# A hybrid trunk layer on one core: in-projection weight loads issued from ScalarE's queue, norm sums later, last activations kept in SBUF

## The chip, the cores and the metric

One core of a Trainium2 chip runs one program. The time of a run is device microseconds of that program; the time of a kernel is the median of its runs. The kernel before took 1511.74 us (three runs: 1519.3, 1505.03 and 1511.74).

## The reference

One layer over a sequence of 1024 steps and 1024 channels, in float32, and a last norm:

```python
h = rmsnorm(x, ln1_g[l])
p = h @ w_in[l]
pm, pr, pw = jnp.split(p, [M_COLS, M_COLS + R_COLS], axis=-1)
ym = mlstm_group(pm, ...)
yr = retention_group(pr)
yw = rwkv7_group(pw, ...)
y = jnp.concatenate([ym, yr, yw], axis=-1).astype(x.dtype)
x = x + y @ w_out[l]
h = rmsnorm(x, ln2_g[l])
x = x + (jax.nn.silu(h @ w_gate[l]) * (h @ w_up[l])) @ w_down[l]
...
return rmsnorm(x, lnf_g)
```

`rmsnorm` divides by the root of the mean square over the channels. The hidden width D_FF is 2816, 22 blocks of 128. The three groups are recurrences over time: mLSTM with 4 heads, retention with 6, RWKV-7 with 6, of 64 channels each.

## The kernel before, in words

**Precision.** Every operand of a large product is kept as two numbers, hi and lo. `split_hi` (L89, one ScalarE activation at L90) rounds to fp32r, `split_lo` (L92, one VectorE subtraction at L93) takes the rest, and a product is three matmuls: hi by hi, hi by lo, lo by hi. In the profile the weights are `whi` and `wlo`, the activations `act` and `act2`.

**Weight loads.** `w_part` (L99 to L102) takes one of three buffers named `wraw`, issues a load of 256 KB on SP's queue (L101), and returns it; `w_split` (L104) makes whi and wlo. A buffer is free for the next load when VectorE has made its wlo. The loads of w_cm and w_tm (the columns of w_in by channel and by time), of w_out and of w_down pass here, 210 in all. Gate and up weights have buffers of their own, `rg`, two of 1 MB, which the loads of hidden activations in the last stage use too.

**Stages.** Time is cut into two halves h of 512 steps, held as free elements of a tile; the partitions are channels.

1. From 0 to about 760 us: in-projection, the three mixers, and the out-projection of half 0. The order of the work is made by `weave` (L131, called at L1127), which takes generators in turn by a clock of its own and by named events; the instructions then run in that order on each engine. In the RWKV part, `rwkv_chain` carries a state over chunks (L581 to L600: matmuls into `chain`, copies `pm` at L583, `X` at L592 and L593 and `yw` at L610 on ScalarE). `rwkv_inverse` (L500) solves triangular systems: E goes to DRAM as `ab_d` (L497), comes back as `MN` (L507), is copied to `R` on ScalarE (L509), is worked on by VectorE (L514 to L522), and goes by `r_d` (L528) back into E (L532). It runs six times; every one of these transfers is issued on SP. So are the stores of the token-wise projections (`v_dram`, L760).
2. From about 760 to 830 us: the out-projection of half 1 (`out_tile`, L1033), eight tiles of 24 matmuls (L119 to L121) with steps of two generators put between each six matmuls: `second_norm(0)` (L1068) and `first_half`, which prepares operands for the next stage. `second_norm` has `rms_stats` (L155: matmuls of the summed squares `sqa` with ones at L159, a mean `ms` on VectorE at L161, a power `rs` on POOL at L162) and, two steps later, `rms_expand` (L164: matmuls at L166 that spread the factors to `misc`) and a copy to `RS`. The summed squares come from POOL (L1049). `second_half(d)` (L1154) makes further operands of tile d by subtractions on POOL and VectorE and by splits. After the last tile the first products of gate and up begin (`product`, L1171 to L1173), with copies named `pre` (L1432) and with the steps of `second_norm(1, 4)` between.
3. From about 830 to 1245 us: gate and up products of a scheme that needs seven products of half-size blocks in place of eight. Each hidden block of a half is stored to `a_dram` (L1181), but for the last two blocks of half 0, which stay in SBUF: `DIRECT` (L1185).
4. From about 1245 us to the end: the down-projection, for each half eight tiles of 22 x 3 matmuls (L1364 to L1366 into `chain`). `take` (L1307) makes its operands: it loads four blocks at a time from `a_dram` into `rg` (L1324) and splits them in pairs, or splits the tiles kept in SBUF. The residuals come back as `x3` (L1359), in buffers shared with the `work` tiles of stage 3.

**Order of the queues.** On each engine instructions run in program order, and a transfer waits on the queue of the engine that issues it: what stands behind it there waits too.

## Time and profile before

| what | us |
|---|---|
| median of three runs | 1511.74 |
| lowest and highest | 1505.03, 1519.3 |
| the profiled execution, its own time | 1521.67 |
| its span | 1519.9 |
| TensorE (PE) busy | 1425.6 |
| VectorE (DVE) busy | 892.4 |
| ScalarE (ACT) busy | 556.2 |
| GpSimd (POOL) busy | 437.9 |

The profile is one execution. A row of a group or a timeline names the line, the engine, the operation and what it writes and reads; a number in brackets is how long the engine sat idle before it and what ended that. PEld is the loading of TensorE's stationary operand, beside the matmuls. SPq and ACTq are issues of transfers. The granted clock is the share of full speed that TensorE was given: at full clock 512-column matmuls follow each other by 0.23 us, at half clock (0.50) by 0.43.

### The profile page before, as it was taken

The page shows a single profiled execution, that of the slowest core. Times are in us where ns is not written, and L with a number is a line of the kernel's source. Part 1 is how long each engine was busy: PE and PEld are TensorE (multiplying, and loading weights), DVE is VectorE, ACT ScalarE, POOL GpSimd, SP SyncE. Part 2 cuts the span into 40 slices and gives each one's busy share as a digit, 9 for nine tenths or more (in the row PEclk, how much of TensorE's full clock was granted, in tenths as well). Part 3 has the DMA queues.
Part 4 walks back from the last instruction along what each step waited for, and adds up shares of the span by engine and source line. Part 5 has one row for each costly group of instructions (what it writes and reads, how often), then busy time and mean ns, then how long its engine had stood idle before and what let it go on. Part 6 is the DMA issues. An engine that isn't in the chain of part 4 may idle for free.

```text
span 1519.9 us, 23085 instructions
## 1 busy us (share of the span) xinstructions
PE 1425.6 (94%) x8434; PEld 1161.3 (76%) x8434; DVE 892.4 (59%) x1762; ACT 556.2 (37%) x1202; POOL 437.9 (29%) x539
## 2 busy tenths in 40 slices
PE   7998799789998998999998999999999998999996
PEld 5777577777777887887777887888888886887886
DVE  6457567458847756645468555555555565347434
ACT  6353334333432133244456333333333344224222
POOL 3211013234424333333545433344444420000000
PEclk9999999999978889899999999999999999999998
DMA  5142122334422244354632222222222247337333
GB/s 209 43 136 66 50 80 74 83 89 112 122 59 68 85 129 124 106 161 142 220 112 85 96 83 83 72 73 78 83 84 83 83 168 255 93 95 238 98 97 111
DMA packets 122269, 164.55 MB, mean 108 GB/s; under 512 B 38028, under 2 KB 70956, under 8 KB 120876
## 3 DMA queue, kind: packets, MB, share of 16 engines
q1 hardware_dynamic: 122156, 163.08, 33.5%
q8 instruction: 66, 1.08, 0.3%
q14 instruction: 47, 0.39, 0.1%
HBM read 124.75 MB, written 38.29 MB: 107 GB/s over the span
## 4 chain that ended last, share of the span: by engine, by line
PE 53%; DVE 3%; POOL 2%; DMA 2%; issue 1%; ACT 0%; POOLq 0%; DVEq 0%; SPq 0%; ACTq 0%
PE acc L1171 5%; PE acc L1172 5%; PE acc L1173 5%; PE chain L1365 5%; PE chain L1364 5%; PE chain L1366 5%; PE misc L1172 4%; PE misc L1171 4%; PE misc L1173 4%; PE acc L119 2%; PE acc L121 2%; PE acc L120 2%; DVE act L93 1%; PE acc L729 1%; PE acc L731 1%
## 5 line engine op out<-in xcount | busy, mean ns | idle before, releaser
L93 DVE TENSOR_TENSOR wlo<-wraw,whi 128x512 fp32r<-128x512 f32 (+1 forms) x210 | 147.9, 707 | 138.3 <-ACT whi L90 137.1
L90 ACT ACTIVATE whi<-wraw 128x512 fp32r<-128x512 f32 (+1 forms) x210 | 128.1, 612 | 226.3 <-PE chain L1365 117.9
L729 PE MATMUL acc<-whi,act 128*128 128x256 f32 (+1 forms) x512 | 161.3, 318 | 4.4 <-ACT whi L90 3.4
L90 ACT ACTIVATE whi<-rg 128x512 fp32r<-128x512 f32 x128 | 79.8, 631 | 228.7 <-POOL rg L1232 90.0
L730 PE MATMUL acc<-wlo,act 128*128 128x256 f32 (+1 forms) x512 | 155.4, 305 | 5.2 <-DVE wlo L93 5.2
L119 PE MATMUL acc<-act,whi 128*128 128x512 f32 x352 | 152.3, 433 | 7.0 <-ACT whi L90 6.2
L93 DVE TENSOR_TENSOR wlo<-rg,whi 128x512 fp32r<-128x512 f32 x128 | 93.1, 728 | 108.1 <-ACT whi L90 105.9
L731 PE MATMUL acc<-whi,act 128*128 128x256 f32 (+1 forms) x512 | 153.0, 300 | 0.0
L1364 PE MATMUL chain<-act,whi 128*128 128x512 f32 (+1 forms) x374 | 144.3, 386 | 4.0 <-ACT act L90 4.0
L120 PE MATMUL acc<-act,whi 128*128 128x512 f32 x352 | 145.5, 413 | 1.5 <-DVE act L252 1.5
L121 PE MATMUL acc<-act,wlo 128*128 128x512 f32 x352 | 145.7, 414 | 1.1 <-DVE wlo L93 1.1
L1365 PE MATMUL chain<-act,whi 128*128 128x512 f32 (+1 forms) x374 | 144.0, 385 | 0.5 <-DVE act L93 0.5
L1366 PE MATMUL chain<-act,wlo 128*128 128x512 f32 (+1 forms) x374 | 143.8, 384 | 0.0
L1171 PE MATMUL acc<-act,whi 128*128 128x512 f32 x352 | 139.3, 396 | 3.4 <-ACT pre L1432 2.7
L1173 PE MATMUL acc<-act,wlo 128*128 128x512 f32 x352 | 138.8, 394 | 0.0
L1172 PE MATMUL acc<-act,whi 128*128 128x512 f32 x352 | 138.5, 394 | 0.0
L729 PEld LDWEIGHTS acc<-whi,act 128*128 128x128 f32 x512 | 104.3, 205 | 12.1 <-ACT whi L90 3.9
L730 PEld LDWEIGHTS acc<-wlo,act 128*128 128x128 f32 x512 | 105.0, 206 | 9.2 <-DVE wlo L93 6.7
L731 PEld LDWEIGHTS acc<-whi,act 128*128 128x128 f32 x512 | 105.2, 206 | 1.0
L1172 PE MATMUL misc<-act,whi 128*128 128x512 f32 x264 | 104.1, 394 | 0.0
L1171 PE MATMUL misc<-act,whi 128*128 128x512 f32 x264 | 104.0, 394 | 0.0
L1173 PE MATMUL misc<-act,wlo 128*128 128x512 f32 x264 | 103.8, 393 | 0.0
(327 smaller groups left out, 2835.9 us busy)
## 6 DMA issues: line engine op xcount, KB each, us to landing
wraw<-in_w_down SPq DMA_DIRECT2D x85, 256.0 KB, 2.7
rg<-in_w_gate SPq DMA_DIRECT2D x22, 512.0 KB, 4.9
rg<-in_w_up SPq DMA_DIRECT2D x22, 512.0 KB, 5.0
a_dram<-work SPq DMA_DIRECT2D x41, 256.0 KB, 2.2
wraw<-in_w_tm SPq DMA_DIRECT2D x40, 256.0 KB, 3.0
rg<-a_dram SPq DMA_DIRECT2D x10, 1024.0 KB, 6.1
v_dram<-vt SPq DMA_DIRECT2D x64, 128.0 KB, 1.9
wraw<-in_w_out SPq DMA_DIRECT2D x32, 256.0 KB, 3.2
```

The source lines that it names most:

```text
L90: S.activation(hi, src, AF.Copy, scale=scale)
L93: (eng or V).tensor_tensor(lo, src, hi.bitcast(F32), ALU.subtract)
L119: PE.matmul(ps, lhsT=hi, rhs=xh[:, k, :], start=(k == 0), stop=False)
L729: PE.matmul(o, lhsT=xh[h][:, k, sl], rhs=w[k][0], start=(k == 0), stop=False)
L730: PE.matmul(o, lhsT=xh[h][:, k, sl], rhs=w[k][1], start=False, stop=False)
L731: PE.matmul(o, lhsT=xl[h][:, k, sl], rhs=w[k][0], start=False, stop=(k == KT - 1))
L1171: PE.matmul(ps, lhsT=hi, rhs=hi_x[:, k, :], start=(start and k == 0), stop=False, skip_group_check=True)
L1172: PE.matmul(ps, lhsT=hi, rhs=lo_x[:, k, :], start=False, stop=False, skip_group_check=True)
L1173: PE.matmul(ps, lhsT=lo, rhs=hi_x[:, k, :], start=False, stop=(stop and k == 3), skip_group_check=True)
L1364: PE.matmul(ps, lhsT=hi, rhs=hi_a[:, sl], start=(f == 0), stop=False)
L1365: PE.matmul(ps, lhsT=hi, rhs=lo_a[:, sl], start=False, stop=False)
L1366: PE.matmul(ps, lhsT=lo, rhs=hi_a[:, sl], start=False, stop=(f == FT - 1))
```

## The change

It has four parts. All line numbers behind L101 grow by two or more.

- While `weave` runs, weight loads are issued on ScalarE's queue in place of SP's: 84 loads of 256 KB (w_cm, w_tm and the w_out tiles of half 0). The first four, those of the out-projection of half 1 and those of w_down stay on SP.
- `second_norm` has four steps, not two, between the sums and their expansion, for both halves; and for half 0 it begins after four steps, not one.
- Four hidden blocks of half 0 (18 to 21) stay in SBUF, not two. Two stores of 256 KB go, and a load of 1 MB (blocks 16 to 19) becomes one of 512 KB. `take` is written anew for blocks partly kept and partly loaded.
- `second_half` of the last tile is issued right after the first `pre` copy.

```diff
+    queue = [SY]
+
     def w_part(src):
         raw = w_tile(*src.shape[1:], "wraw", F32, WRAW)
-        SY.dma_start(out=raw, in_=src)
+        queue[0].dma_start(out=raw, in_=src)
         return raw
...
         rms_stats(const, [sqa2[h]], 4, f"b{h}", rs)
-        yield
-        yield
+        for _ in range(4):
+            yield
         pr = misc_tile()
...
+    queue[0] = S
     weave([rwkv_chain(), rwkv_inverse(), rwkv_prep(), rwkv_out(), norms(), attention()],
           [rwkv_proj(), fillers(), out_proj()])
+    queue[0] = SY
...
-        DIRECT = (FT - 2, FT - 1)
+        DIRECT = range(FT - 4, FT)
...
-                n = min(4, gs.stop - f)
-                if h == 0 and f in DIRECT:
-                    for y in range(f, f + n):
-                        o = y - gs.start
-                        split_hi(hi[:, o, :], direct[y])
-                        split_lo(lo[:, o, :], direct[y], hi[:, o, :])
-                        ah[h, y] = hi[:, o, :], lo[:, o, :]
-                    continue
-                r = sb.tile([P, 4, HF], F32, name="rg", tag="rg", bufs=2)
-                SY.dma_start(out=r[:, 0:n, :], in_=a_dram[h][:, f:f + n, :])
...
+                here = [y for y in range(f, min(f + 4, gs.stop)) if h == 0 and y in DIRECT]
+                n = min(4, gs.stop - f) - len(here)
+                if n:
+                    r = sb.tile([P, 4, HF], F32, name="rg", tag="rg", bufs=2)
+                    SY.dma_start(out=r[:, 0:n, :], in_=a_dram[h][:, f:f + n, :])
+                parts = [(f + z, 2, r[:, z:z + 2, :]) for z in range(0, n, 2)] + [(y, 1, direct[y].unsqueeze(1)) for y in here]
+                for y, m, src in parts:
+                    o = slice(y - gs.start, y - gs.start + m)
+                    split_hi(hi[:, o, :], src)
+                    split_lo(lo[:, o, :], src, hi[:, o, :])
...
-        between = chain(second_norm(0), first_half())
+        between = chain(second_norm(0, 4), first_half())
...
-        second_half(KT - 1)
         steps = second_norm(1, 4)
...
-                S.copy(out=pre[j, m], in_=ps[m])
+                copy = S.copy(out=pre[j, m], in_=ps[m])
+                if j == m == 0:
+                    with tc.issue_after(copy.ins):
+                        second_half(KT - 1)
```

**Where instructions move.** Three places. The first is TensorE at the beginning of the out-projection of half 1, before: acc_8241 is its first tile, whi_8221 and whi_8225 the two parts of that tile's weights, of 12 matmuls each; rows between the threes of a part are left out.

```order
L119 MATMUL acc_8241<-act_7382,whi_8221 128x512
L120 MATMUL acc_8241<-act_7383,whi_8221 128x512
L121 MATMUL acc_8241<-act_7382,wlo_8222 128x512
L159 MATMUL misc_8255<-ones1_135,sqa2_7527 128x1 x4
L119 MATMUL acc_8241<-act_7382,whi_8225 128x512
L120 MATMUL acc_8241<-act_7383,whi_8225 128x512
L121 MATMUL acc_8241<-act_7382,wlo_8226 128x512
L166 MATMUL misc_8275<-cst_112,rs0_8254 128x128 x4
```

And now, where acc_8291 is the second tile and acc_8351 the third; six matmuls of whi_8233 stand ahead of the sums and six of whi_8283 ahead of the expansion:

```order
L123 MATMUL acc_8241<-act_7382,wlo_8226 128x512
L121 MATMUL acc_8291<-act_7382,whi_8233 128x512
L122 MATMUL acc_8291<-act_7383,whi_8233 128x512
L123 MATMUL acc_8291<-act_7382,wlo_8234 128x512
L161 MATMUL misc_8299<-ones1_135,sqa2_7527 128x1 x4
L123 MATMUL acc_8291<-act_7382,wlo_8238 128x512
L121 MATMUL acc_8351<-act_7382,whi_8283 128x512
L168 MATMUL misc_8358<-cst_112,rs0_8298 128x128 x4
```

The sums (L159, now L161) stood behind 12 matmuls of the first tile and stand now behind 30, and 24 matmuls, not 12, lie between them and the expansion (L166, now L168).

The second place is ScalarE around the end of the first inverse, in the first stage, now (tq and E are the inverse's copies, X, yw, pm the chain's):

```order
L90 ACTIVATE whi_1605<-wraw_1599 128x512
L103 DMA wraw_1868<-in_w_cm 128x512
L545 COPY tq_1268<-misc_1345 32x256 x2
L551 COPY E_685<-misc_1345 32x8x32 x2
L594 COPY X_580<-chain_1406 64x64
L595 COPY X_580<-chain_1406 64x64
L337 ACTIVATE t_1477<-rp_1473,omu_137 128x512
L612 COPY yw_1400<-chain_1406 128x64
```

Before, the load of wraw_1868 stood on SP, behind the transfers that bring the first inverse back into E:

```order
L528 DMA r_d_1261<-R_792 4x256x32
L507 DMA MN_1436<-ab_d_1256 128x1x1024
L101 DMA wraw_1709<-in_w_cm 128x512
L532 DMA E_685<-r_d_1261 32x8x32 x4
L101 DMA wraw_1868<-in_w_cm 128x512
```

It has moved between a split and the copies of the inverse and the chain on ScalarE, and is gone from between the inverse's transfers on SP.

The third place is SP at the start of the down-projection, before (x3 the residuals, rg_11736 blocks 12 to 15, rg_11812 blocks 16 to 19):

```order
L1359 DMA x3_11818<-x2_dram0_192 128x512 x6
L1324 DMA rg_11700<-a_dram0_8201 128x2048
L1359 DMA x3_11818<-x2_dram0_192 128x512 x2
L1324 DMA rg_11706<-a_dram0_8201 128x2048
L1324 DMA rg_11730<-a_dram0_8201 128x2048
L101 DMA wraw_11820<-in_w_down 128x512
L1181 DMA a_dram1_8202<-work_11509 128x512
L101 DMA wraw_11840<-in_w_down 128x512
L101 DMA wraw_11862<-in_w_down 128x256
L1324 DMA rg_11736<-a_dram0_8201 128x2048
L1324 DMA rg_11812<-a_dram0_8201 128x2048
```

and now:

```order
L1323 DMA rg_11698<-a_dram0_8201 128x2048
L1323 DMA rg_11704<-a_dram0_8201 128x2048
L1323 DMA rg_11728<-a_dram0_8201 128x2048
L103 DMA wraw_11820<-in_w_down 128x512
L1185 DMA a_dram1_8202<-work_11507 128x512
L103 DMA wraw_11840<-in_w_down 128x512
L103 DMA wraw_11862<-in_w_down 128x256
L1323 DMA rg_11734<-a_dram0_8201 128x2048
L1323 DMA rg_11810<-a_dram0_8201 128x1024
L1359 DMA x3_11818<-x2_dram0_192 128x512
L103 DMA wraw_11880<-in_w_down 128x512
L1359 DMA x3_11818<-x2_dram0_192 128x512 x5
```

The residual loads have moved from ahead of the hidden activations to behind them, because their buffer is held by the blocks that stay in SBUF, and the last of the loads, now rg_11810, is half as large.

More of the change, by code (lines that the diff above doesn't have):

```diff
@@ L1314, in take @@
             for f in range(gs.start, gs.stop, 4)[parts or slice(None)]:
-                n = min(4, gs.stop - f)
-                if h == 0 and f in DIRECT:
-                    for y in range(f, f + n):
-                        o = y - gs.start
-                        split_hi(hi[:, o, :], direct[y])
-                        split_lo(lo[:, o, :], direct[y], hi[:, o, :])
-                        ah[h, y] = hi[:, o, :], lo[:, o, :]
-                    continue
-                r = sb.tile([P, 4, HF], F32, name="rg", tag="rg", bufs=2)
-                SY.dma_start(out=r[:, 0:n, :], in_=a_dram[h][:, f:f + n, :])
-                for z in range(0, n, 2):
-                    o = f - gs.start + z
-                    split_hi(hi[:, o:o + 2, :], r[:, z:z + 2, :])
-                    split_lo(lo[:, o:o + 2, :], r[:, z:z + 2, :], hi[:, o:o + 2, :])
-                    for y in range(o, o + 2):
-                        ah[h, gs.start + y] = hi[:, y, :], lo[:, y, :]
+                here = [y for y in range(f, min(f + 4, gs.stop)) if h == 0 and y in DIRECT]
[8 more added lines that the diff above has]
+                    split_lo(lo[:, o, :], src, hi[:, o, :])
+                    for z in range(m):
+                        ah[h, y + z] = hi[:, o.start + z, :], lo[:, o.start + z, :]
         x3 = {}
```

## The prediction

> **What bounds the kernel now.** I read the page first, then busy time by stage (four windows: in-projection with the mixers, out-projection of the second half with the transition, gate/up, down-projection), then the waits of TensorE by stage.
>
> ```profile
> span 1519.9 us, 23085 instructions
> PE 1425.6 (94%) x8434; PEld 1161.3 (76%) x8434; DVE 892.4 (59%) x1762; ACT 556.2 (37%) x1202; POOL 437.9 (29%) x539
> ...
> 0.00:760.00 760.00, 691.55 (x5215) 565.63 (x5216) 477.72 (x1184) 288.45 (x758) 236.80 (x401) 0.92 0.35 108
> 760.00:830.00 70.00, 61.88 (x269) 49.75 (x268) 56.47 (x68) 42.48 (x72) 35.76 (x23) 0.95 0.30 98
> 830.00:1245.00 415.00, 414.24 (x1787) 334.98 (x1786) 225.65 (x310) 136.80 (x236) 158.73 (x111) 1.00 0.25 87
> 1245.00:1520.00 275.00, 257.94 (x1168) 210.90 (x1166) 132.54 (x202) 88.45 (x138) 6.58 (x5) 0.97 0.46 143
> ```
>
> The windows' columns are PE, PEld, DVE, ACT and POOL busy, granted clock, DMA share, GB/s. TensorE sets the time; gate/up has nothing to give. Whatever the change is worth must come out of TensorE's idle time in the other three stages and out of the half clock that follows it. Its waits in the first 745 us, then around the transition, then at the start of the down-projection:
>
> ```profile
> PE misc L540 <- DVE tq L535: 10.5, 3, 7.7
> PE chain L597 <- ACT X L593: 7.8, 3, 6.0
> PE chain L586 <- ACT pm L583: 7.6, 5, 2.0
> PE acc L119 <- ACT whi L90: 6.2, 1, 6.2
> PE misc L460 <- DVE E L468: 5.2, 3, 4.3
> PE acc L730 <- DVE wlo L93: 5.2, 7, 1.7
> PE chain L581 <- DVE X L607: 4.4, 1, 4.4
> PE acc L729 <- ACT whi L90: 3.4, 2, 3.0
> ...
> PE misc L159 <- POOL sqa L1049: 3.8, 1, 3.8
> PE acc L1171 <- ACT pre L1432: 2.7, 2, 1.6
> PE misc L166 <- POOL rs L162: 1.6, 1, 1.6
> ...
> PE chain L1364 <- ACT act L90: 4.0, 1, 4.0
> ```
>
> (Columns: total us, times, longest.) The change can touch four of these: the waits on wlo and whi at L730 and L729 (8.6 us), the norm sums' wait (3.8), their expansion's (1.6) and the down-projection's first (4.0). The 6.2 us at L119 is the first weight of all, whose load stays on SP. The rest belongs to the RWKV chain.
>
> **Norm sums, first half.** TensorE's timeline, the chain that ended last, and a window:
>
> ```profile
> 760.69 0.39 PE L120 MATMUL acc<-act,whi 128*128 128x512 f32 x1
> 760.92 0.39 PE L121 MATMUL acc<-act,wlo 128*128 128x512 f32 x1
> 765.10 1.87 PE L159 MATMUL misc<-ones,sqa 128*128 128x1 f32 x8 [3.79 <-POOL sqa L1049]
> 771.24 0.39 PE L120 MATMUL acc<-act,whi 128*128 128x512 f32 x1
> ...
> 761.66 1.72 POOL s1x L1206
> 763.38 1.68 POOL sqa L1049
> ...
> 765.10:771.20 6.10, 6.10 (x18) 5.18 (x19) 4.69 (x6) 0.01 (x1) 5.92 (x4) 0.50 0.00 0
> ```
>
> Without the wait, the sums would start at 760.92 + 0.23 (the step between the first two rows) = 761.15, take half of 1.87 at full clock (0.94), and ten matmuls of 0.23 would bring TensorE at 764.39 to where it is at 771.24: 6.85 us are lost, 3.8 to the wait and the rest to the half clock behind it. In the new order the sums stand 18 matmuls later: 761.15 + 18 x 0.23 = 765.29, and POOL's last addition ends at 763.38 + 1.68 = 765.06. That leaves 0.23 us to spare, so the stall goes, barely. The expansion stands 24 matmuls (5.5 us) behind the sums, and ends up at 771.7 as before, so that no reader of RS gets it later. I take 6.5 gained, as POOL could be some tenths later; the ends are 6.85 and 3.8 (if a rest of the wait keeps the half clock, only the idle time comes back).
>
> **Norm sums, second half.** The sums stay in their place and the expansion moves from 12 to 24 matmuls behind them, 12 x 0.23 = 2.8 us, more than the 1.6 us it waits. Gain 1.65; ends 1.65 and nothing (if the matmuls pulled ahead wait for operands themselves, as at L1171).
>
> **second_half(7) after the first `pre` copy.** On ScalarE and VectorE each of its instructions has the same neighbours in both orders. Nothing; the 2.7 us at L1171 stay.
>
> **Activations kept in SBUF.** The first wait of the down-projection is for block 12 to 15:
>
> ```profile
> 1251.48 0.37 SPq L1324 DMA_DIRECT2D rg<-a_dram  x1
> ...
> 1247.18 6.23 DVE L93 TENSOR_TENSOR act<-rg,act 128x1024 fp32r<-128x1024 f32 x4
> ...
> 1259.39 2.00 ACT L90 ACTIVATE act<-rg 128x1024 fp32r<-128x1024 f32 x2 [2.90 <-DMA rg<-a_dram]
> ...
> rg<-a_dram SPq DMA_DIRECT2D x10, 1024.0 KB, 6.1
> ```
>
> That load is issued when VectorE has split half of what lies in the two rg buffers (the second of four splits from 1247.18 ends near 1250.3), and the change alters neither the buffers nor those splits. So the wait stays. It took 7.9 us to arrive, against a median of 6.1, beside the 1 MB load of block 16 to 19, which becomes 512 KB; but the eight residual loads of 256 KB, done before, now come into the same time. If the traffic saved wins, 1.8 us come back; if the moved loads win, I allow 1.5 lost, half of what one 256 KB load takes (3.0 below). The four splits replace as many bytes of rg splits. Value: gain 0.7.
>
> **Weight loads on ScalarE's queue.** SP's waits in the first 745 us, what one load costs its issuer (min/median/max ns), and ScalarE's longest waits there:
>
> ```profile
> SPq L101 <- DVE wlo L93: 119.2, 36, 16.0
> SPq L101 <- DVE R L522: 29.4, 10, 13.0
> SPq L101 <- DVE rt L519: 13.0, 6, 4.6
> SPq L507 <- DMA ab_d<-E: 4.3, 3, 2.0
> ...
> L101 SPq DMA_DIRECT2D wraw<-in_w_tm x44: 327/333/968, 43.6 to 662.1; - x44
> ...
> DMA to landing us min/median/max: 2.5/3.0/8.9
> ...
> ACT yw L610 <- DVE X L607: 62.8, 24, 10.1
> ACT X L592 <- PE chain L590: 49.6, 34, 4.4
> ACT pm L583 <- PE chain L581: 49.5, 27, 8.9
> ACT R L509 <- DMA MN<-ab_d: 27.9, 5, 8.1
> ```
>
> SP spends 161.6 us of the first stage waiting for wraw buffers that VectorE must free. The loads are thus bound by buffers, not by SP's issue time, and on ScalarE they wait for the same buffers. *Gain:* a load that SP holds back behind other transfers can go earlier; at the most all 8.6 us of waits on wlo and whi. I take 4, about half. *Cost:* 84 x 0.33 = 28 us of ScalarE, which is busy for 288 of 760, and the waits that move to it. What is queued behind a waiting load there are the copies X, pm, yw of the RWKV chain and the next whi, for which TensorE waits. Bounds: nothing, if ScalarE would have idled anyway (its waits above are some 190 us), and 42.4 us, if every wait during an inverse (R L522, rt L519) reached TensorE. The first row is nearest: where a load stands behind its whi on ScalarE, VectorE's wlo follows directly. I take 1. Net gain 3; ends 8.6 gained and 42.4 lost, the second only as a rival.
>
> The Trainium skill ("Trainium Kernel Development and Optimization", Key Constraints) says that transfers from SP, ACT and POOL run on the same 16 DMA engines and that several issuers only save issue time. By that rule no transfer gets quicker, and the step would be worth nothing beyond queueing; the trace, where everything is issued from SP, can't show it.
>
> **Sum.** The profiled execution took 1521.67 us (span 1519.9). 6.5 + 1.65 + 0.7 + 3 = 11.85, so 1509.8 for such an execution. It lies 9.9 above the median of the runs (1511.74), and taking the same 11.85 off that gives 1499.9: I predict **1500**.
>
> **Rivals.**
>
> *The freed SP is worth much more (25%).* SP's 161.6 us of waits also stood ahead of the RWKV chain's own small transfers. If these come earlier, the stage's chain stalls shrink: tq, X, pm, E, X above are 35.5 us, and a granted clock of 0.92 over 760 us is 122 us at half clock, 61 lost. A fifth of the 105 (with the 8.6) is 21; with 8.85 from the other parts the time is 1482. Against: at L507, the load on which each inverse hangs, SP waited only 4.3 us, for data, and ScalarE's 27.9 for MN is transfer time.
>
> *Slower: ScalarE stands still (9%).* A weight load whose buffer is held through an inverse blocks ScalarE in order; the copy behind it (X or pm) is late, and TensorE idles with it, then runs at half clock. At the ten waits on R L522 alone this is 29.4: 1511.74 - 8.85 + 29.4 = 1532. It makes the kernel slower from 8.85 us of added idle time on, and by over 1% from 24. For it: 13.0 us in a single wait. Against: in an inverse ScalarE mostly waits too. The skill ("Perfetto Trace Analysis", DMA Instruction — HWDGE) says that the DMA engines don't wait on semaphores on TRN2, so by it the wait is the issuing engine's; the SP rows above agree (16.0 us in one).
>
> *The stalls only move (17%).* TensorE reaches the next limit earlier and waits there:
>
> ```profile
> 800.00:825.00 25.00, 22.31 (x100) 17.73 (x99) 24.19 (x24) 15.29 (x28) 16.67 (x11) 1.00 0.30 96
> ```
>
> VectorE is busy for 24.19 of these 25 us. If its work there can't start earlier, the 8.15 us of the norm sums are given back at L1171, and with a first stage unchanged only 0.7 remains: 1511. Against: over 760 to 830 VectorE has 13.5 us free, and most of what it does follows TensorE's tiles.
>
> **How the numbers follow.** The forecast has 49%, bigger gain 25, moved stalls 17, slower 9. A measurement of this kernel can tell about 1% (15 us) from no change; the three runs alone span 14. Faster by over 1% is the first rival and a quarter of the forecast's cases, 0.37; slower 0.09; within 1% the rest, 0.54. The range, 1482 to 1514, takes in the forecast's own ends (6.85 + 1.65 + 1.8 + 8.6 = 18.9 gained, 1493; 3.8 - 1.5 with nothing from the loads, 1509), the moved stalls, and half of the first rival.
>
> **What would show it.** Right: the 3.79 us before L161 gone and no half clock at 765; no wait before L168 in the second half; the wait of 4 us at the first down chain still there; the first stage within 5 us of its length. Wrong: ScalarE's copies ended by a DMA issue and new TensorE waits on X or pm (slower), or MN loads and inverses markedly earlier and a granted clock of 0.94 or more in the first stage (faster).

## The result and the profile after

The changed kernel took 1508.93 us, the median of 20 runs (1498.81 to 1515.87); the kernel before, in 20 runs beside them, 1519.59 (1505.03 to 1534.38). The ratio is 0.9936, 95% interval 0.9919 to 0.9953: 9.7 us less, between 7.1 and 12.3. Gains in us are always this ratio's share of the time before; the two medians beside it are 10.7 apart. The ratios leave out runs that are over 1.5% above the fastest of their kernel, here one of the kernel before, and below at most one of a kernel but for three of the twelve with w_cm back on SP. The three runs of the kernel before that the prediction starts from had a median of 1511.74, 7.9 below that of the 20.

Busy time by stage in the changed kernel, in the same windows as before (PE, PEld, DVE, ACT, POOL, granted clock, DMA share, GB/s):

```profile
span 1509.5 us, 23051 instructions
...
0.00:760.00 760.00, 693.43 (x5250) 563.32 (x5251) 485.37 (x1188) 295.24 (x769) 243.11 (x405) 0.94 0.36 109
760.00:830.00 70.00, 65.25 (x280) 52.70 (x279) 57.48 (x69) 37.73 (x64) 30.63 (x21) 0.95 0.33 109
830.00:1245.00 415.00, 414.36 (x1786) 334.90 (x1785) 231.09 (x315) 141.86 (x242) 161.23 (x112) 1.00 0.24 83
1245.00:1510.00 265.00, 247.66 (x1123) 202.73 (x1121) 122.30 (x193) 81.17 (x128) 2.81 (x3) 0.97 0.47 146
```

The windows are fixed in time, so work has slid between them. Read by events instead, the profile of the changed kernel is ahead of the other by 7.0 us at VectorE's addition of the last out-projection tile of half 0 (751.56, before 758.60), by 10.5 once the first pair of gate and up runs (the 181st product matmul, the 61st of L1171, now L1175), and by 10.4 at its end. So the first stage gave 7.0 us in these two executions, the transition 3.5, the down-projection nothing.

TensorE's waits around the transition and at the start of the down-projection, now:

```profile
PE acc L1175 <- ACT pre L1431: 2.7, 1, 2.7
PE misc L168 <- POOL rs L164: 2.0, 1, 2.0
...
PE chain L1364 <- ACT act L90: 3.5, 1, 3.5
PE chain L1365 <- DVE act L93: 0.8, 1, 0.8
```

(The chain matmuls have the line numbers L1364 to L1366 in both kernels, as `take` became shorter.) The 3.8 us before the sums are gone, and so are the 1.6 before half 1's expansion. A wait of 2.0 us before half 0's expansion is new, the two waits on `pre` are one of 2.7, and the down-projection's first wait is what it was (3.5 + 0.8, before 4.0 + 0.5). The timelines of TensorE, VectorE and POOL show the new wait:

```profile
758.31 0.95 PE L161 MATMUL misc<-ones,sqa 128*128 128x1 f32 x8
766.93 1.16 PE L168 MATMUL misc<-cst,rs 128*128 128x128 f32 x8 [2.04 <-POOL rs L164]
...
760.06 1.78 DVE L93 TENSOR_TENSOR wlo<-wraw,whi 128x512 fp32r<-128x512 f32 x1
761.76 2.37 DVE L93 TENSOR_TENSOR act<-x,act 128x512 fp32r<-128x512 f32 x2
764.05 0.68 DVE L1043 TENSOR_TENSOR x<-x,acc 128x512 f32<-128x512 f32 x1
764.65 0.68 DVE L93 TENSOR_TENSOR wlo<-wraw,whi 128x512 fp32r<-128x512 f32 x1
765.25 0.15 DVE L163 TENSOR_SCALAR ms<-misc 128x4 f32<-128x4 f32 x1
...
765.48 1.40 POOL L164 TENSOR_TENSOR rs<-ms,neghalf 128x4 f32<-128x4 f32 x1 [2.50 <-DVE ms L163]
```

The sums are done at 759.1, but the mean of 0.15 us stands on VectorE behind two weight splits, two operand splits and an addition, and comes at 765.25. Then POOL needs 1.40, and TensorE has run out of the 24 matmuls. Before, the sums came so late that VectorE had run out of work, and it took the mean at once; rs then came behind three operations on POOL, 4.2 us after the sums' end (766.97 to 771.18), which the twelve matmuls at half clock covered:

```profile
767.01 0.16 DVE L161 TENSOR_SCALAR ms<-misc 128x4 f32<-128x4 f32 x1 [1.41 <-PE misc L159]
769.72 1.46 POOL L162 TENSOR_TENSOR rs<-ms,neghalf 128x4 f32<-128x4 f32 x1
```

### The profile page after: what moved, and what is told of

Its sections match the earlier page's. It is cut to its first block, busy times and chain, and to the rows that moved or that the text cites. A ratio compares the mean times of both kernels' runs of the same rounds, so it can differ in the third digit from the quotient of the medians.

```text
span 1509.5 us, 23051 instructions
## 1 busy us (share of the span) xinstructions
PE 1420.7 (94%) x8434; PEld 1153.6 (76%) x8434; DVE 896.2 (59%) x1763; ACT 556.0 (37%) x1203; POOL 437.8 (29%) x539
## 4 chain that ended last, share of the span: by engine, by line
PE 67%; DVE 10%; DMA 9%; issue 3%; ACT 2%; POOL 2%; SPq 0%; DVEq 0%; POOLq 0%; ACTq 0%
PE acc L1175 5%; PE acc L1176 5%; PE acc L1177 5%; PE chain L1365 5%; PE chain L1364 5%; PE chain L1366 5%; PE acc L121 4%; PE misc L1176 4%; PE misc L1175 4%; PE misc L1177 4%; PE acc L122 4%; PE acc L123 4%; DMA MN<-ab_d 3%; DMA r_d<-R 2%; PE acc L732 2%
## 5 line engine op out<-in xcount | busy, mean ns | idle before, releaser
L93 DVE TENSOR_TENSOR wlo<-wraw,whi 128x512 fp32r<-128x512 f32 (+1 forms) x210 | 152.6, 731 | 132.7 <-ACT whi L90 131.6
L731 PE MATMUL acc<-whi,act 128*128 128x256 f32 (+1 forms) x512 | 157.6, 310 | 4.3 <-ACT whi L90 3.3
L733 PE MATMUL acc<-whi,act 128*128 128x256 f32 (+1 forms) x512 | 150.3, 295 | 0.0
L1364 PE MATMUL chain<-act,whi 128*128 128x512 f32 (+1 forms) x374 | 144.4, 386 | 3.5 <-ACT act L90 3.5
L1366 PE MATMUL chain<-act,wlo 128*128 128x512 f32 (+1 forms) x374 | 144.3, 386 | 0.0
L1175 PE MATMUL acc<-act,whi 128*128 128x512 f32 x352 | 140.3, 399 | 3.3 <-ACT pre L1431 2.7
L731 PEld LDWEIGHTS acc<-whi,act 128*128 128x128 f32 x512 | 101.3, 199 | 11.6 <-ACT whi L90 3.9
L732 PEld LDWEIGHTS acc<-wlo,act 128*128 128x128 f32 x512 | 101.6, 199 | 9.9 <-DVE wlo L93 7.1
L1175 PE MATMUL misc<-act,whi 128*128 128x512 f32 x264 | 104.0, 394 | 0.0
L733 PEld LDWEIGHTS acc<-whi,act 128*128 128x128 f32 x512 | 101.9, 199 | 1.1
```

Source lines behind the costliest of these rows:

```text
L93: (eng or V).tensor_tensor(lo, src, hi.bitcast(F32), ALU.subtract)
L731: PE.matmul(o, lhsT=xh[h][:, k, sl], rhs=w[k][0], start=(k == 0), stop=False)
L732: PE.matmul(o, lhsT=xh[h][:, k, sl], rhs=w[k][1], start=False, stop=False)
L733: PE.matmul(o, lhsT=xl[h][:, k, sl], rhs=w[k][0], start=False, stop=(k == KT - 1))
L1175: PE.matmul(ps, lhsT=hi, rhs=hi_x[:, k, :], start=(start and k == 0), stop=False, skip_group_check=True)
L1364: PE.matmul(ps, lhsT=hi, rhs=hi_a[:, sl], start=(f == 0), stop=False)
```

## The experiments

Times are against the kernel before, run beside each version on the same chip; lengths of stages are from one profile each, and there are 20 profiles in all. The first stage ends at the addition named above, the transition at the 181st product matmul.

### The parts by themselves

**Only the queue**, measured twice.

```diff
-        SY.dma_start(out=raw, in_=src)
+        queue[0].dma_start(out=raw, in_=src)
...
+    queue[0] = S
     weave(...)
+    queue[0] = SY
```

> Only the queue of the weight loads is changed. Theory: most of the gain of the whole change is here. In the two profiles the first stage (to the last out-projection tile of half 0, VectorE's eighth addition of that stage) became 7.0 us shorter, above all because MN of the sixth inverse was issued 2.6 us and landed 3.4 us earlier on an SP queue without weight loads; so -5 to -9 us against the kernel before, -0.3 to -0.6%. Rival: the 7 us are scatter of the half clock between two executions, and the queue is worth nothing; then within 2 us, and the first stage's length as before within its scatter.

Measured: 1514.27 against 1516.79, ratio 0.9978 (0.9945 to 1.0011).

> Only the queue of the weight loads, again, since the first measurement (ratio 0.9978, interval 0.9945 to 1.0011) leaves it open. Theory: a small gain, 0.2 to 0.35% (3 to 5 us), as the difference between the whole change and the change without the queue says too. Rival: nothing; then the ratio comes out above 0.998 and the two measurements together hold 1. Spread of the first stage between executions of one program is some 12 us, so that single profiles can't decide it.

Measured: 1512.95 against 1518.99, ratio 0.996 (0.9937 to 0.9982). The gains are 3.3 and 6.1 us; the first interval reaches over 1, the second doesn't. That the first stage's 7.0 us in the two profiles are this gain doesn't follow: with the same program of that stage, it took 758.6, 754.2, 747.0, 756.8 and 768.9 us in five profiles (loads on SP) and 751.6, 753.7, 747.5, 759.4, 753.2 and 761.3 in six (loads on ScalarE). Single profiles differ by up to 22 us; the means, 757.1 and 754.4, are 2.7 apart.

**Only the norm sums** (four steps ahead of the sums of half 0, four between sums and expansion).

> Only the norm sums are moved (four steps before the sums of half 0, four between sums and expansion). Theory: the 3.79 us before the sums go with their half clock (6.85), but the expansion of half 0 now waits about 2 us for POOL's power, since VectorE computes the mean only behind its splits, and around 808 to 818 the waits on pre grow together and bring half clock; so -3 to -5 us. Rival (the sum as predicted): -8 us, both waits gone with nothing in their place.

Measured: 1509.45 against 1516.79, ratio 0.997 (0.9948 to 0.9992), 4.6 us less. The transition took 97.05 us, in the kernel before 101.61. Its waits:

```profile
PE acc L1171 <- ACT pre L1432: 2.7, 2, 1.6
PE misc L166 <- POOL rs L162: 2.3, 1, 2.3
```

The theory holds as far as half 0's expansion, with 2.3 us of new wait; the rival, nothing in the place of the old waits, is out. That the waits on `pre` grow together, as the theory also said, isn't seen here. The lengths of the transition bear the 4.6 us out, though single times differ by 1%: 101.3 to 102.7 us in the eight profiles with the old norm sums (mean 101.9), 96.0 to 98.2 in nine of the ten with the new ones and nothing else altered there (mean of all ten 97.4; the tenth, with w_cm back on SP, took 101.5).

**Only the blocks kept in SBUF.**

> Only the four blocks are kept in SBUF. Theory: the first wait of the down-projection (4.0 + 0.5 us) stays within half a us, its load being bound by the rg buffers; 0 to -1 us in all. Rival (traffic decides): the load of blocks 12 to 15 arrives 1.8 us earlier and the time falls by 2 us or more.

Measured: 1516.1 against 1516.79, ratio 1.0003 (0.9979 to 1.0027). Nothing.

**All but the queue**, measured twice.

> The whole change but for the queue: weight loads stay on SP. Theory: the parts add, so -3 to -5 us, as with the norm sums alone, and the first stage as long as in the kernel before. Rival (queue worth nothing): the full -9.7 us of the whole change.

Measured: ratio 0.9971 (0.9945 to 0.9997).

> The whole change but for the queue, again, on the same chip as the run beside it. Theory (the queue gains a little): 0.997 as before, short of the 0.9936 of the whole change. Rival (the queue gains nothing): at or below 0.995, as the whole change.

Measured: ratio 0.9965 (0.9938 to 0.9991). Both are what the norm sums alone bring, and short of the whole change, though their intervals reach into its. Here `second_half` is moved and in "only the norm sums" it isn't: the transition took 96.7 and 97.0 us against 97.1, so that part is worth nothing. In the first of the two profiles the sums still waited 1.0 us for POOL's `sqa`, and the expansion for nothing. Queue (0.22 and 0.40%) and norm sums (0.30%) add up to the whole (0.64%).

### Whose queue, and which loads

**MN alone on ScalarE's queue**, the weights on SP.

```diff
-                SY.dma_start(out=MN, in_=ab_d...
+                S.dma_start(out=MN, in_=ab_d...
```

> The kernel before, with one line changed: MN, the load on which each of the six inverses hangs, is issued from ScalarE's queue (whose next copies read it anyway); the weight loads stay on SP. In the profile of before, MN was issued 0.2, 7.3, 5.5, 2.4, 3.7 and 3.1 us after the last ab_d transfer that it reads had landed, 22 us in all. Theory: in the whole change these 22 us shrank only to 21, so the small gain of the weight queue (0.2 to 0.35%) doesn't come from MN; taking SP out of its way brings at most 3 us, since the second inverse also waits for its buffer. Rival (the freed SP is what counts, through the inverse): the inverses come up to 3 us earlier each, the stalls on tq and X shrink, and the time falls by 8 us or more.

Measured: 1530.01 against 1517.73, ratio 1.0056 (1.0024 to 1.0087): slower by 8.5 us. Neither theory nor rival had that. One wait of TensorE in the first stage is new, and at the second inverse r_d is late. TensorE's wait, a row of ScalarE just before it, and MN and r_d:

```profile
PE acc L729 <- ACT GT L737: 5.5, 1, 5.5
...
116.11 1.66 ACT L509 COPY R<-MN 32x256 f32<-32x256 f32 x4 [6.11 <-DMA MN<-ab_d]
...
146.56 0.52 ACTq L507 DMA_DIRECT2D MN<-ab_d  x1
147.95 0.68 SPq L528 DMA_DIRECT2D r_d<-R  x1
157.91 2.03 SPq L532 DMA_DIRECT2D E<-r_d  x4
```

GT stands behind the copies of R, and these wait 6.1 us for the first MN to land, before 2.6: what holds ScalarE here is not MN's issue but the copy that reads it, which the new order put ahead of other work. At the second inverse MN goes 1.4 us ahead of r_d, and E, which needs r_d and waits for it to the last, is issued 10.0 us after it, before 4.8. From the first r_d to the second the profile has 45.5 us, before 36.5; that is 9.0 of the 13.2 us by which the first stage is longer in these two profiles. This place comes back below.

**The weight loads on POOL's queue.**

```diff
-    queue[0] = S
+    queue[0] = G
```

> The whole change, with the 84 weight loads on POOL's queue and not on ScalarE's. Theory: as the whole change within 4 us (about -10 us against the kernel before) if what counts is only that the loads leave SP. Rival (a cost of waiting on ScalarE, hidden in the small gain): on POOL, which does little for TensorE's next step, the gain is larger by 4 us or more. Third possibility: POOL's own work (vt, st, hh) is held by the waiting loads, and the time rises above that of the kernel before.

Measured: 1529.24 against 1517.73, ratio 1.0054 (1.0024 to 1.0084): 18 us behind the whole change's ratio. POOL's waits in the first 745 us:

```profile
POOL wraw L103 <- DVE wlo L93: 54.4, 20, 5.7
```

The third possibility in the time: POOL stands 54.4 us before held buffers, the issues keep it busy for 0.55 to 0.59 us each (279.18 us in the first 760, in the changed kernel 243.11), and the first stage takes 774.8 us. So leaving SP is not enough. That POOL's waiting is what costs the time is argued, not shown.

**Only w_cm, only w_tm, only w_out of half 0** on ScalarE's queue (the other loads on SP, the rest as in the kernel before).

```diff
+        keep, queue[0] = queue[0], SY
         ws = ws or [load_w(a["w_cm"][idx], V) for idx, _ in tiles]
+        queue[0] = keep
```

> The kernel before with only the w_cm loads of the first stage (those for the channel-wise projections, mostly in the first 370 us, where the first three inverses are) on ScalarE's queue. Theory: these loads are where ScalarE stands longest before a held buffer (9.4 us at the worst place), and they bring nothing or lose: 0.999 to 1.003. Rival (each load that leaves SP brings its share): a quarter to a third of the queue's gain, 0.998 to 0.999; or all of it, 0.996 to 0.998.

Measured: 1522.92 against 1519.12, ratio 1.0045 (1.0023 to 1.0067), slower by 6.8 us.

> The kernel before with only the w_tm loads (token-wise projections, 44 to 662 us) on ScalarE's queue. Theory: the queue's gain (0.3%) is here, for here SP held loads 2 to 7 us behind stores of v_dram and the inverse's transfers in the trace of before: 0.995 to 0.998. Rival: the gain is spread or elsewhere, 0.999 or more.

Measured: 1514.73, ratio 0.9966 (0.9941 to 0.999), faster by 5.2.

> The kernel before with only the w_out loads of half 0 (666 to 743 us) on ScalarE's queue. Theory: TensorE waits in that stretch for weights only once (0.6 us), so nothing: 0.999 to 1.001. Rival: SP's stores for retention are late there behind the loads, and the out-projection starts earlier: 0.997 to 0.998.

Measured: 1519.07, ratio 1.0002 (0.9984 to 1.002). Nothing.

So the w_tm loads carry the gain, and the w_cm loads lose. The three don't add up to the queue as a whole (1.6 us slower, against 3.3 and 6.1 faster), which their intervals of some 3 us each way leave open. The traces show one place for each. **The gain, at the sixth inverse.** SP in the kernel before, and in the changed one:

```profile
577.96 2.15 SPq L497 DMA_DIRECT2D ab_d<-E  x4
580.70 0.35 SPq L101 DMA_DIRECT2D wraw<-in_w_tm  x1
583.89 0.34 SPq L760 DMA_DIRECT2D v_dram<-vt  x1
584.40 0.53 SPq L507 DMA_DIRECT2D MN<-ab_d  x1
```

```profile
578.31 2.15 SPq L499 DMA_DIRECT2D ab_d<-E  x4
581.83 0.54 SPq L509 DMA_DIRECT2D MN<-ab_d  x1
584.15 5.33 SPq L762 DMA_DIRECT2D v_dram<-vt  x2
```

Before, a weight load and then a store that waits for vt stand ahead of MN; without the loads the order on SP changes too, and the store comes behind. MN goes 2.6 us earlier, and TensorE's wait on X at that place (chain matmul from X) is 6.0 us before, 5.5 with w_cm alone, 4.9 with w_out alone, but 3.0 with w_tm alone, and 2.5 in the changed kernel (first before, then w_tm alone):

```profile
PE chain L597 <- ACT X L593: 6.0, 1, 6.0
```

```profile
PE chain L601 <- ACT X L597: 3.0, 1, 3.0
```

It is so in every profile: 4.9 to 6.0 us in the seven with w_tm and MN on SP, 2.5 to 3.3 in the eleven with w_tm on ScalarE, and 6.2 with the loads on POOL. At the end of that inverse a second piece is gained. In those seven r_d is issued 3.0 us after VectorE's last step, for it waits for POOL, which in the kernel before writes its part of R behind three other operations; in those eleven it is 0.35 us. The fifth and the sixth r_d, before and in the changed kernel:

```profile
521.61 0.56 SPq L528 DMA_DIRECT2D r_d<-R  x1
634.70 0.54 SPq L528 DMA_DIRECT2D r_d<-R  x1
```

```profile
522.07 0.56 SPq L530 DMA_DIRECT2D r_d<-R  x1
627.72 0.54 SPq L530 DMA_DIRECT2D r_d<-R  x1
```

They lie 113.1 us apart before and 105.7 in the changed kernel. In the seven it is 111.6 to 113.1 and in the eleven 105.5 to 108.6, in the mean 6.1 less; with the loads on POOL 116.1. That is about the gain that w_tm alone has (5.2).

**The loss, at the second inverse.** SP before, and in the changed kernel, with SP's wait for the first inverse's way back and TensorE's wait on tq:

```profile
148.54 0.56 SPq L528 DMA_DIRECT2D r_d<-R  x1
149.28 2.15 SPq L507 DMA_DIRECT2D MN<-ab_d  x1
153.33 1.81 SPq L532 DMA_DIRECT2D E<-r_d  x4
...
SPq L532 <- DMA r_d<-R: 1.4, 1, 1.4
...
PE misc L540 <- DVE tq L535: 7.7, 1, 7.7
```

```profile
145.78 0.56 SPq L509 DMA_DIRECT2D MN<-ab_d  x1
146.51 0.53 SPq L530 DMA_DIRECT2D r_d<-R  x1
158.02 1.79 SPq L534 DMA_DIRECT2D E<-r_d  x4
...
SPq L534 <- DMA r_d<-R: 11.0, 1, 11.0
...
PE misc L542 <- DVE tq L537: 8.5, 1, 8.5
```

MN, 512 KB, now goes ahead of r_d, 128 KB, and r_d lands so late that E is issued 11.5 us after it (158.02 - 146.51) and not 4.8 (153.33 - 148.54). Tq of the first inverse, for which TensorE waits, hangs on E. With w_cm alone on ScalarE this wait is 9.1 us, with w_tm alone 7.5. Again it is so in every profile: 8.5 to 10.2 us in the eight with MN ahead of r_d on SP, 6.8 to 8.1 in the eleven with r_d ahead. More than the wait is lost: the granted clock from 150 to 200 us is 0.83 in the changed kernel, before 0.93. The second r_d, before and in the changed kernel:

```profile
185.06 0.55 SPq L528 DMA_DIRECT2D r_d<-R  x1
```

```profile
187.97 0.54 SPq L530 DMA_DIRECT2D r_d<-R  x1
```

It comes 36.5 us after the first before, and 41.5 now. With r_d ahead this stretch takes 36.0 to 40.9 us, with MN ahead 41.5 to 45.2; the means, 37.7 and 43.1, are 5.4 apart. ScalarE's own long wait here in the changed kernel, 10.0 us, is at the copy of R, for r_d, and not at a weight load: the load in front of it is issued at 148.84.

The Trainium skill ("DMA: Bandwidth & Descriptors", Queues, rings and completion order) says that each DMA engine takes what one issuer sent it in the order of its ring. The 11.0 us behind MN and the 1.4 us ahead of it are in line with that. But with MN alone on ScalarE, another issuer, E was issued 10.0 us after r_d as well; so that the ring makes r_d late isn't shown, only that an MN issued ahead of it does.

**w_cm back on SP** in the whole change.

> The whole change with the w_cm loads (the ones around the first inverses) back on SP; those of w_tm and w_out stay on ScalarE. Theory: the small gain of the queue is the difference of a gain (loads and stores no longer behind each other on SP) and a loss (ScalarE stands before a load whose buffer the inverse holds, 9.4 us at the worst place, which is a w_cm load); without that place the gain is 2 to 4 us larger: -12 to -14 us. Rival: ScalarE idles at that place in any case; then as the whole change (-10), or less gain, as fewer loads leave SP.

Measured: 1509.45 against 1518.99, ratio 0.9913 (0.9884 to 0.9943): 13.2 us, as the theory has it, though its interval reaches over the ratio of the whole change. The ratio rests on nine runs; over all twelve the medians (1509.45 and 1518.99) are 9.5 us apart, as much as the whole change brings. So this run doesn't decide between theory and rival.

**MN kept behind r_d** in the whole change, all loads on ScalarE.

```diff
+                with ExitStack() as behind:
+                    if rd:
+                        behind.enter_context(tc.issue_after(rd[-1].ins))
-                SY.dma_start(out=MN, in_=ab_d...
+                    SY.dma_start(out=MN, in_=ab_d...
...
-                SY.dma_start(out=r_d...
+                rd.append(SY.dma_start(out=r_d...))
```

> The whole change, with MN of an inverse kept behind r_d of the one before on SP's queue (all weight loads of the stage stay on ScalarE). In the whole change the second MN (512 KB) was issued 0.7 us ahead of the first r_d, which then landed 11 us later and not 4.8; before, a weight load stood between and the order was r_d, MN. Theory: this order, not ScalarE's waiting, is what the w_cm loads cost; r_d is waited for 1 to 2 us again and not 11, TensorE's wait on tq goes from 8.5 to some 7.5 us, and the time falls by 2 to 7 us below the whole change (0.989 to 0.992). Rival (ScalarE waiting before held buffers is the cost): the wait on tq may shrink, but the time stays as in the whole change, 0.993 to 0.994.

Measured: 1506.2 against 1518.64, ratio 0.9926 (0.9896 to 0.9955). In its profile:

```profile
SPq L538 <- DMA r_d<-R: 1.8, 1, 1.8
...
PE misc L546 <- DVE tq L541: 7.4, 1, 7.4
```

The waits do what the theory says: 1.8 in place of 11.0, and 7.4 in place of 8.5. The time is 1.5 us below the whole change's, less than these measurements can tell apart. But the stretch from the first r_d to the second is 36.0 us here and 36.3 in the other version with this order (below), with every load still on ScalarE. So the order of MN and r_d is what costs the 5.4 us at that place, and ScalarE's waiting isn't; it is most of the 6.8 us that w_cm alone costs. That the whole time follows by as much isn't shown.

### The new waits

**The expansion of half 0 later by 12 matmuls**, in the whole change.

```diff
-        for _ in range(4):
+        for _ in range(4 if h else 6):
             yield
```

> The whole change, with the expansion of half 0's norm factors 36 matmuls behind the sums and not 24. Theory: the 2.04 us before the expansion are VectorE computing the mean behind its splits; 12 matmuls more (2.8 us) hide them, and -2 us against the whole change follow (-11 to -12 against the kernel before). Rival (VectorE is the limit of the whole stage): the 2 us come back before the first pre copy, and nothing is gained.

Measured: 1512.26 against 1517.73, ratio 0.9945 (0.9915 to 0.9975). TensorE's waits in the transition:

```profile
PE acc L1175 <- ACT pre L1431: 4.3, 2, 3.3
PE acc L1177 <- DVE wlo L93: 0.8, 1, 0.8
```

The wait for rs is gone, and 0.8 us on a weight split and 1.6 more on `pre` have taken its place. In the time the rival holds, as nothing is gained. The transition took 95.6 us, 0.4 to 1.5 less than in the six profiles with the new norm sums that stayed at full clock after `pre` (96.0 to 97.1), so a part of the 2 us may be left.

**Kept blocks first**, in the first tile of the down-projection.

```diff
+            groups = [(f, min(f + 4, FT)) for f in range(0, FT, 4)]
+            if h == d == 0:
+                groups = [(0, 4), (4, 8), (8, 12), (18, 22), (16, 18), (12, 16)]
...
+            elif i == last - 4:
+                take(0, 1, slice(0, 1))
+            elif i == last - 1:
+                take(0, 2, slice(0, 1))
+            elif i == last + 1:
+                take(0, 2, slice(1, 2))
+                take(0, 1, slice(1, 2))
```

> The whole change, and in the first tile of the down-projection of half 0 the blocks kept in SBUF (18 to 21) and then 16 and 17 are multiplied before 12 to 15, whose load is issued last (the sum of one tile is added in another order). Theory: the first wait of the down-projection (3.5 + 0.75 us and half clock behind it, 7.3 us lost in all) is the arrival of blocks 12 to 15; 18 matmuls in between (4.2 us) hide most of it, and 4 to 7 us are gained against the whole change (-14 to -17 against the kernel before). Rival (VectorE's splits are late, not the load): the wait comes back before the kept blocks, and less than 2 us are gained.

Measured: 1507.63 against 1517.73, ratio 0.9932 (0.99 to 0.9964). From the first matmul of the down-projection to its 121st it took 31.6 us and not 35.4, and one wait is left there:

```profile
PE chain L1370 <- DVE wlo L93: 2.6, 1, 2.6
```

The load of blocks 12 to 15 was the cause of the old wait; what is left is a weight split behind block splits on VectorE. In all four versions with this order the 121 matmuls take 31.3 to 32.6 us, in the other 16 profiles 33.7 to 35.5. The ratio alone shows 0.6 us against the whole change and not the 4 to 7 that were expected.

This program and the changed kernel are alike in the transition, and both have VectorE at 14.00 of 14 us around the first `pre` copy. First this kernel, then the changed one:

```profile
804.00:818.00 14.00, 10.68 (x49) 8.21 (x49) 14.00 (x17) 10.28 (x20) 8.71 (x6) 1.00 0.23 75
```

```profile
802.00:816.00 14.00, 11.29 (x41) 9.02 (x40) 14.00 (x17) 10.12 (x20) 8.72 (x6) 0.78 0.23 75
```

Here TensorE was granted 1.00, there 0.78: 49 matmuls against 41 in the same 14 us. That makes 2 us of difference in the transition (96.08 and 98.12). The first wait on `pre` doesn't tell which of the two comes: in nine of the 20 profiles the granted clock is 0.50 to 0.74 in the 6 us behind it, and the wait was 2.06 to 3.35 us; in the other eleven the clock is 1.00, and it was 1.65 to 3.35. These eleven have a second wait on `pre` of 1.0 us, some 5 us later, and the nine have none. So it looks as if the half clock makes one wait of two, by bringing TensorE later to the second place, and not as if the single wait brought the half clock. What brings it, no run here shows.

**Eight lo splits on POOL**, on top of the new order.

```diff
-                    split(n, k, z[:, k0 + k, :])
+                    split(n, k, z[:, k0 + k, :], G)
```

> The whole change with the new order of blocks in the first down tile, and with the eight lo splits of the last operands (products 7 and 4 of the first pair) on POOL and not on VectorE. Theory: VectorE, busy without a gap for some 20 us around the first pre copy, is what TensorE waits for there; with 4.8 us of its work gone the waits on pre (2.3 + 1.0 or 2.7 in one) and on the mean shrink by 2 us or more, on top of the 3.8 us that the new order saved at the down-projection: -14 to -16 us against the kernel before. Rival: POOL takes 1.7 us for what VectorE does in 0.6, and its subtractions for the later operands come late behind them; then TensorE waits for products 7 and 4 instead, and nothing is gained at the transition.

Measured: 1508.49 against 1518.99, ratio 0.9936 (0.9909 to 0.9963), no better than without. Its profile is its slowest run (1522.9). The waits of the transition in its profile are 3.4 on `pre`, 2.0 on rs and 1.4 on a weight split, and VectorE is busy for 59.3 of the 70 us. The theory falls; that POOL's own work comes late, as the rival says, wasn't seen either.

**The versions that measured best, together**: w_cm on SP and kept blocks first, and then MN behind r_d and kept blocks first.

> The whole change with w_cm back on SP and with the new order of blocks in the first down tile: the two versions that measured best, together. Theory (both hold, and add): 0.988 to 0.991, -14 to -18 us against the kernel before. Rival (the version with w_cm on SP was lucky): as the whole change with the new order alone, 0.993.

Measured: 1501.97 against 1519.12, ratio 0.9897 (0.987 to 0.9925), 15.6 us less.

> The same with the new order of blocks in the first down tile. Theory: as the version with w_cm on SP and the new order (0.9897), or better, since w_cm's loads need not stand on SP: 0.987 to 0.990. Rival (w_cm on ScalarE costs something besides the order of MN and r_d): 0.992 to 0.994.

Measured: 1500.93 against 1518.64, ratio 0.9907 (0.9871 to 0.9944), 14.1 less. Both beat the kernel before. Against the changed kernel (0.9936, from 0.9919) neither is clear: the first one's interval ends at 0.9925, the second's at 0.9944, and each has six runs. Between the two nothing is decided.

## Why the prediction was right or wrong

| step | predicted, us | measured, us |
|---|---|---|
| norm sums, both halves | -8.15 | -4.6 (alone) |
| `second_half` after the first `pre` copy | 0 | 0 (transition 96.7 and 97.0 with it, 97.1 without) |
| blocks kept in SBUF | -0.7 | +0.5, interval -3.2 to +4.1 |
| queue of the weight loads | -3 | -3.3 and -6.1 (alone) |
| sum | -11.85 | -9.7 |
| starting time | 1511.74 | 1519.59 |

The direction stands, and the size of three of the four steps. The 8.9 us between 1500 and 1508.93 are 7.9 of the starting time, which was taken from three runs that happened to lie low, and about 1 of the sum (2.1 by the ratio). The prediction had the profiled execution at 1521.67 beside that median and chose the lower; its sum for "such an execution", 1509.8, is within 2 us of the changed kernel's profiled one (1511.56). Behind that bad luck, one term of the sum was too large, and one had the right size by luck.

**The step that failed is the norm sums**, 8.15 us in the sum and 4.6 measured (1.2 to 7.9). "The stall goes, barely" is right: no wait is left before L161 in the changed kernel, 1.0 us in one of its variants. Wrong is the sentence after it, that the expansion would stand where it stood in time and wait for nothing. The prediction counted the matmuls between sums and expansion (24, 5.5 us) and not the way of the result: VectorE's mean stands behind some 6 us of splits, and POOL's power takes 1.4. In the kernel before the way was shorter, 4.2 us, since VectorE stood idle when the sums came, and the twelve matmuls took 4.9 at half clock (766.83 to 771.70). Now it is 7.6 us against 5.5 of cover. Of the 6.5 us, 2.0 went here (2.3 with the norm sums alone).

The second half's 1.65 us were rightly seen to go. The rival "the stalls only move" came in part: a little under half of the 8.15 us was lost, but not at L1171, where the waits on `pre` are 2.7 us before and in the changed kernel. It was lost at the expansion, for a mean that stands behind VectorE's splits, and in some executions to half clock behind `pre`. Only when the expansion was moved further did waits on `pre` and a weight split take the place of its wait, with VectorE busy for 14.00 of 14 us there in the changed kernel.

**Blocks in SBUF:** right for the reason given: the load of blocks 12 to 15 still waits for the rg buffers, and its split starts 7.3 us after its issue (1241.15 to 1248.47) and not 7.9. That less traffic and the residual loads moved beside it cancelled isn't shown by itself. Taking the load out of the way (kept blocks first) removed the wait, which shows that it was the load.

**The queue:** the size was right by luck, and the reasons were not. TensorE's waits on wlo and whi, of which the prediction took 4 of 8.6 us as gained, are 8.4 in the changed kernel. What the traces show is a gain of 6.1 us around the sixth inverse (MN ahead of a waiting store, and POOL's part of R sooner) and a loss of 5.4 at the second (MN ahead of r_d). These two nearly cancel, so where the rest of the 3.3 and 6.1 us comes from stays open; the first stage scatters by more than that. A granted clock of 0.94 in that stage, which the prediction has as a sign of the larger gain, was seen (0.92 before) without that gain. The first rival named that way of gaining, and argued from the 4.3 us in the waits at L507 that there was little in it. That row counts only the time in which MN itself was at the head of the queue. The time that it stood behind others is in the rows of those others: 3.1 us there, from the landing of ab_d at 581.3 to the issue at 584.40. And the prediction listed earlier MN loads as a sign of gain, where at the second inverse the earlier MN was the loss.

The Trainium skill's rule ("Trainium Kernel Development and Optimization", Key Constraints), that several issuers only save issue time, would have made the step worth nothing beyond queueing. The measurements show what queueing is worth: the order on the queues changed, and with it the time, -0.34% for w_tm, +0.45% for w_cm, and +0.54% for the whole change with all loads on POOL. For the other page ("Perfetto Trace Analysis", DMA Instruction — HWDGE), by which the issuing engine does the waiting, the trace agrees on SP, where 11.0 us of waiting for r_d are at the line of E's loads. The slower rival didn't come to pass: where w_cm's loads on ScalarE lose, it is mostly by the order of MN and r_d on SP.

## What to carry to other kernels

When a wait goes because its consumer is moved back, follow the result onward through each engine that touches it, by what stands ahead of it there; a count of TensorE's own instructions is not the cover, and the stall that goes may have kept the way short, by leaving an engine on it idle. A transfer's delay is read from when its data was ready to when it was issued, not from the waits put down to it; moving loads off a queue reorders what is left, and a large load that gets ahead of a small store can cost what the move won. Where executions of one program differ by 1%, no stage of a single profile proves a gain. But a short stretch between two fixed instructions, read in every profile at hand, can: if its lengths with the change and without it don't overlap, the place is found, and its size with it. A start for a forecast is taken from more than three runs.

## What was not expected of the hardware

- Half clock after a short wait, and not always: 2.7 us of idle time, with a granted clock of 0.78 over the 14 us around it; in a program with the same transition waits of 2.3 and 1.0 us and 1.00, and in another 3.3 and 1.0 and 1.00.
- A store of 128 KB issued 0.7 us behind a load of 512 KB on one queue was waited for 11.0 us; issued 0.7 us ahead of it, 1.4. With the load on another engine's queue, 1.4 us ahead, what needed the store was issued 10.0 us after it.
- The whole change with the same 84 loads on POOL is some 18 us slower than with them on ScalarE; POOL has 54.4 us of waiting at them. With them on ScalarE, moving r_d ahead of MN on SP alone takes the stretch from the first r_d to the second from 41.5 us down to 36.0.
